# A PEER expert layer on one core: a second raw buffer for U blocks, and the low halves of V blocks moved from GpSimd to VectorE

## The chip, the cores and the metric

The kernel runs on 1 core of one Trainium2 chip. The metric is the device time of one execution in microseconds (us); less is better. Three runs of the kernel before took 3746.31, 3746.49 and 3755.15 us, a median of 3746.49 us.

The engines are called as the profile calls them: PE is TensorE (PEld its weight loads), DVE is VectorE, ACT is ScalarE, POOL is GpSimd, SP is SyncE, which here only issues DMAs.

## The reference

One layer of a hybrid backbone over 1024 tokens of 1024 channels: adaLN norm, one input projection, a Hyena long convolution beside grouped-query attention, an output projection, and then a PEER layer of single-neuron experts. The change concerns the PEER layer alone:

```python
def chunk(xc):                       # 128 tokens
    q = (xc @ wq).reshape(PEER_CHUNK, PEER_HEADS, 2, half)
    s1 = jnp.einsum('chd,hnd->chn', q[:, :, 0], keys1)
    s2 = jnp.einsum('chd,hnd->chn', q[:, :, 1], keys2)
    ...                              # top 16 of the 128x128 sums per head
    g = jax.nn.softmax(best, axis=-1)
    a = jnp.einsum('chkd,cd->chk', u_tab[eidx], xc)
    wgt = gelu(a) * g
    return jnp.einsum('chk,chkd->cd', wgt, v_tab[eidx])
```

There are 16384 experts, each a row of U and a row of V (1024 float32 numbers, 4 KB). Every token uses 128 of them (8 heads by 16).

## The kernel before

Up to about 1685 us the kernel does everything ahead of the experts. The rest of the program does the expert layer in two ways side by side.

**Dense experts, the main work** (`dense`). The first 640 tokens (`DT` = 5 tiles of 128) meet all 16384 experts. U and V are cut into 128 blocks of 128 experts, and four blocks (`CH`) make a chunk. For each block the kernel loads a transposed U block `ur` (512 KB, issued on SP), and splits it into a rounded high half `uh` on ACT (L90) and a low half `ul` = `ur` - `uh` on DVE (L91); both go to a function `split`. PE then forms the products with the tokens in three passes (high by high, high by low, low by high: L85 to L87), 48 matmuls of 320 columns a block. ACT puts a GELU on the result (`ga`), DVE multiplies it by the gate weights `gt` (L1000), and `wh` and `wl` are its halves. The function `values` loads the V block `vr` (512 KB) and splits it into `vh` (ACT) and `vl`. After four blocks, `products` forms the output of the chunk for each of the five tiles, 24 matmuls of 512 columns a tile, and DVE adds each half of it from PSUM to `acc` (L1022), ten additions a chunk.

The buffers matter here: one `ur` (`UR` = 1), one `vr`, two each of `uh` and `ul`, four each of `vh` and `vl` (`VH`). The constant `VG` = (0, 2) says on which engine `vl` is made: for blocks whose number is 0 or 2 modulo 4 on POOL, for the others on DVE.

**Gathered experts, the background.** For the other 384 tokens (tiles 5 to 7, list `E`) the rows of U and V are gathered by index. POOL issues 128 indirect DMAs a tile for U (`usweep`, L887; one row for each of 128 tokens, 512 KB) and 128 for V (`vrows`, L933). DVE takes the dot product of each U row with its token (L888) and adds each V row, weighted, to a sum in PSUM (L937). `topk` finds the indices. It also transposes them on PE into `eT`, for a function `vsweep`; the list `VD` = (5, 6, 7) sends all three tiles to `vrows`, so that `vsweep` is never run, and `eT` is not read.

`weave` writes background steps among the dense steps at a fixed ratio. The order that each engine then gets is made by the framework's scheduler, which plays the program through on estimated durations. Every engine works strictly in the order it got, and SP issues its DMAs in that order too: an instruction that waits holds up all that stand behind it.

Of the kernel before, what the change touches and what calls it, by code (L numbers as in the profile page):

```python
# [10 lines left out]
F32 = mybir.dt.float32  # L11
F32R = mybir.dt.float32r
I32 = mybir.dt.int32
# [4 lines left out]
PSUM = bass.MemoryType.PSUM  # L18
# [3 lines left out]
D = 1024  # L22
# [30 lines left out]
RUNS = _runs()  # L53
RW = 7
VB = 2
CH, WB, VH, GA, UR = 4, 4, 4, 1, 1
OB, GB = 4, 2
RB, RB0, RBR, MGB = 3, 2, 1.0, 4
O1DVE, OA = (0,), 1
BG0, BGR0 = 200, 2.4  # L60
VG = (0,2)
GB4, MGB4, OA4, OB4 = 2, 2, 1, 3
ND, DC = 2, 23
LR = 3
VD = (5, 6, 7)
BGR = 1.3
DT = 5

# [1 line left out]
def body(tc, d, out, dbg=None):  # L70
# [4 lines left out]
    def pool(name, bufs=1, space=None, stack=es, **kw):  # L75
        if space is not None:
            kw["space"] = space
        if space != DRAM:
            kw["reuse_waits"] = "tile"
        return stack.enter_context(tc.tile_pool(name=name, bufs=bufs, **kw))  # L80
# [12 lines left out]
    with es:  # L93
# [706 lines left out]
        def topk(i, v16, i16, p, res, ps, dense):  # L800
# [50 lines left out]
            efl = ef.rearrange("p h k -> p (h k)")  # L851
            if "eidx" in dbg:
                SY.dma_start(dbg["eidx"][i], efl)
            pt = ps.tile([128, 512], F32, name="ms")
            PE.transpose(pt[:, 0:128], efl, ident)
            if not dense:
                ei = res.tile([128, 128], I32, name=f"ei{i}", bufs=1)
                V.tensor_copy(ei, efl)
                eT = res.tile([128, 128], I32, name=f"eT{i}", bufs=1)
                V.tensor_copy(eT, pt[:, 0:128])  # L860
                tops[i] = gwl, ei, eT
                return
            PE.transpose(pt[:, 128:256], gwl, ident)
            nb = 1 if i == DT - 1 else 2
            gT = res.tile([128, 256], F32, name="gT", bufs=nb)
# [28 lines left out]
            V.tensor_tensor(gw, gw, a, OP.mult)  # L894
            ws[i] = gw

        def vsweep(i, tops, ws, p, gp, ms, ap, res, wdz):
            w, eT = ws[i], tops[i][2]
            pt = ms.tile([128, 512], F32, name="ms")
            PE.transpose(pt[:, :128], w, ident)  # L900
            acc = ap.tile([128, 2, 512], F32, name="acc")
            pv = pt[:, :128].rearrange("p (c t) -> p c t", c=4)
            wT = res.tile([128, 4, 32], F32, name="wT", bufs=1)
            V.tensor_copy(wT, pv)
            for th in range(8):
                V.memset(wdz, 0.0)
                V.tensor_copy(wdz[:, :, th * 4:128:33], wT[:, :, th * 4:th * 4 + 4])
                for tm in range(4):
                    tl = th * 4 + tm
                    vgs = [gp.tile([128, D], F32, name="row", bufs=RW) if c else p.tile([128, D], F32, name="vg", bufs=VB) for c in range(4)]  # L910
                    for c in range(4):
                        G.indirect_dma_start(out=vgs[c], out_offset=None, in_=d["v"], in_offset=bass.IndirectOffsetOnAxis(ap=eT[:, c * 32 + tl:c * 32 + tl + 1], axis=0))
                    lead = None
                    for h in range(2):
                        for c in (3, 0, 1, 2):
                            mm = PE.matmul(acc[c * 32:c * 32 + 32, h, :], wdz[:, c, tm * 32:tm * 32 + 32], vgs[c][:, h * 512:(h + 1) * 512],
                                           start=tl == 0, stop=tl == 31, tile_position=(0, c * 32))
                            if lead is None:
                                lead = mm
                            else:  # L920
                                tc.add_manual_dep(mm.ins, lead.ins.name, mybir.DependencyInfo(mybir.DependencyClass.NoSync, mybir.DependencyReason.DATA), reason="behind the last gather")
                    yield 1
            gt = [gp.tile([128, D], F32, name="row", bufs=RW) for _ in range(4)]
            gates(gt)
            final(i, acc.rearrange("p a b -> p (a b)"), gt[2], gt[3], gt, p)

        def vrows(i, tops, ws, p, gp, ap):

            w, ei = ws[i], tops[i][1]
            acc = ap.tile([128, 2, 512], F32, name="acc").rearrange("p a b -> p (a b)")  # L930
            for s_ in range(128):
                row = gp.tile([128, D], F32, name="h2" if i == 7 else "row", bufs=1 if i == 7 else RW) if s_ % 3 == 1 else p.tile([128, D], F32, name="vg", bufs=VB)
                G.indirect_dma_start(out=row, out_offset=None, in_=d["v"], in_offset=bass.IndirectOffsetOnAxis(ap=ei[:, s_:s_ + 1], axis=0))  # L933
                if s_ == 0:
                    V.tensor_scalar(acc, row, w[:, 0:1], None, OP.mult)
                else:
                    V.scalar_tensor_tensor(acc, row, w[:, s_:s_ + 1], acc, OP.mult, OP.add)  # L937
                if s_ % 4 == 3:
                    yield 1
            gt = [gp.tile([128, D], F32, name="row", bufs=RW) for _ in range(4)]  # L940
            gates(gt)
            final(i, acc, gt[2], gt[3], gt, p)
# [34 lines left out]
        def dense(hTh, hTl, gp):  # L977
# [4 lines left out]
            chunks = [list(range(b, min(b + CH, 128))) for b in range(0, 128, CH)]  # L982
            with ExitStack() as st:
                p = pool("de", 1, stack=st)
                ps = pool("deps", 5, PSUM, stack=st)
                acc = p.tile([128, DT, 2, 512], F32, name="acc")

                def weights(c):
# [79 lines left out]
        def gates(gt):  # L1068
            SY.dma_start(gt[0], modd[3:4, :].to_broadcast([128, D]))
            SY.dma_start(gt[1], d["fin_g"].to_broadcast([128, D]))  # L1070
# [43 lines left out]
        with ExitStack() as sg:  # L1114
# [19 lines left out]
            with ExitStack() as sk:  # L1134
# [6 lines left out]
                for _ in rest(0, 4, rps, rwp, tkv, ra, hq):  # L1141
                    pass
                v16, i16, hTh, hTl = ra
                ms = pool("ms", 1, PSUM, stack=sg, side="right")
                def weights_of(tiles, v16, i16, pools, on_act, gb):
                    bp, mg, tk, st_ = pools
                    for i in tiles:
# [22 lines left out]
                with ExitStack() as sb:  # L1170
                    for _ in weights_of(DD[4:], v16, i16, pools(sb, 4, MGB4), OA4, GB4):
                        pass
                gp = pool("gp", 1, stack=sg, side="right")
                sl = ExitStack()
                tk = pool("tk2", 1, stack=sl, side="right")
# [1 line left out]

                def background():
                    def tk_(i):
                        return topk(i, v16[:, i % 4], i16[:, i % 4], tk, res, ms, False)  # L1180

                    yield from tk_(E[0])
                    for i in E[1:]:
                        yield from alternate(tk_(i), first(us[0], 24))
                    sl.close()
                    vp = pool("vp", 1, stack=sg, side="right")
                    ap = pool("ap", 1, PSUM, stack=sg, side="right")
                    wdz = vp.tile([128, 4, 128], F32, name="wdz")
                    vs = [vsweep(i, tops, ws, vp, gp, ms, ap, res, wdz) for i in E if i not in VD]
                    vs += [vrows(i, tops, ws, vp, gp, ap) for i in VD]  # L1190
                    yield from us[0]
                    for j in range(len(E) - 1):
                        yield from alternate(us[j + 1], vs[j])
                    yield from vs[-1]
# [105 lines left out]
```

## Time and profile before

| what | value |
|---|---|
| median of three runs | 3746.49 us |
| the profiled execution: its own time | 3752.46 us |
| the profiled execution: span of the trace | 3750.7 us |
| mean granted TensorE clock | 0.949 |
| first `ur` issued, last `ur` issued | 1685.1 us, 3692.9 us |
| first, last U gather started | 1865.3 us, 3282.6 us |
| last V gather started | 3696.6 us |

The profile is of one execution. Busy time of an engine is the union of its instructions' spans; a group's row gives its count, its busy time, the mean time of one instruction, and then the idle time of the engine just before them with what ended it. In a list of waits, a row names the waiting engine and line, what it waited for, the total, how often, and the longest. Times within the span are counted from its start.

### The profile page before, as it was taken

What the parts mean: (1) busy time and instruction counts of PE and PEld (TensorE: products, weight loads), DVE (VectorE), ACT (ScalarE), POOL (GpSimd) and SP (SyncE); (2) the same over time, 40 slices, a digit from 0 to 9 for tenths busy, and PEclk for the clock granted to TensorE, in tenths of its full rate; (3) what the DMA queues carried; (4) which work ended last, traced back from release to release, by engine and by line L of the source; (5) the groups of instructions that cost most, each with busy time, mean ns of one, the idle gap of its engine ahead of it and who ended that gap; (6) DMA issues with size and microseconds to landing.
All of it is one profiled execution on the core that took longest, in us unless ns stands there. A gap on an engine that the chain in (4) does not pass through costs nothing.

```text
span 3750.7 us, 53277 instructions
## 1 busy us (share of the span) xinstructions
PE 3369.1 (90%) x19601; PEld 2948.2 (79%) x19601; DVE 2879.9 (77%) x5428; ACT 1445.1 (39%) x2966; POOL 1709.2 (46%) x1360
## 2 busy tenths in 40 slices
PE   5899999789999886998889998999999999799998
PEld 2787888567887676888778888988888888687887
DVE  4655554574446899999897989898898989787777
ACT  5543422446565268885511222222232222122222
POOL 0233133220421465104486767676576666544452
PEclk6999999899999998999989999999999999899999
DMA  4554355863322344434488999999999989888886
GB/s 164 176 165 153 129 202 167 294 226 117 110 85 65 104 141 163 167 141 142 165 305 307 322 327 329 337 344 324 335 342 331 325 317 326 286 286 285 264 281 210
DMA packets 334241, 868.31 MB, mean 232 GB/s; under 512 B 31777, under 2 KB 145377, under 8 KB 324764
## 3 DMA queue, kind: packets, MB, share of 16 engines
q0 software_dynamic: 123904, 453.04, 33.9%
q1 hardware_dynamic: 210076, 411.87, 32.4%
q8 instruction: 154, 2.52, 0.3%
q14 instruction: 107, 0.88, 0.1%
HBM read 777.63 MB, written 87.18 MB: 231 GB/s over the span
## 4 chain that ended last, share of the span: by engine, by line
DVE 23%; DMA 16%; PE 14%; issue 8%; POOL 3%; ACT 2%; SPq 0%; DVEq 0%; POOLq 0%; ACTq 0%
PE mm L85 5%; PE mm L86 4%; PE mm L87 4%; DMA vg<-in_v,ei 4%; DMA vr<-in_v 3%; DVE row L888 3%; DVE acc L937 3%; DMA row<-in_u,ei 3%; DMA ur<-in_uT 3%; DVE o L953 2%; DVE o L965 2%; DVE wl L91 1%; DMA h<-in_v,ei 1%; DVE o L963 1%; POOL row L887 1%
## 5 line engine op out<-in xcount | busy, mean ns | idle before, releaser
L85 PE MATMUL mm<-h2Th,uh 128*128 128x320 f32 x2048 | 644.7, 315 | 60.7 <-ACT uh L90 50.3
L87 PE MATMUL mm<-h2Th,ul 128*128 128x320 f32 x2048 | 638.5, 314 | 26.7 <-DVE ul L91 25.8
L86 PE MATMUL mm<-h2Tl,uh 128*128 128x320 f32 x2048 | 641.7, 314 | 0.0
L887 POOL DMA_INDIRECT row<-in_u,ei x384 | 500.4, 1303 | 192.9 <-issue 75.3
L85 PE MATMUL mm<-vh,wh 128*128 128x512 f32 x1280 | 500.6, 404 | 59.6 <-DVE acc L1022 35.9
L888 DVE SCALAR_TENSOR_TENSOR row<-row,h 128x1024 f32<-128x1024 f32 x384 | 508.1, 1341 | 25.1 <-DMA row<-in_u,ei 21.7
L86 PE MATMUL mm<-vl,wh 128*128 128x512 f32 x1280 | 504.3, 401 | 5.8 <-DVE vl L91 3.9
L87 PE MATMUL mm<-vh,wl 128*128 128x512 f32 x1280 | 497.4, 400 | 7.6 <-DVE wl L91 7.5
L85 PEld LDWEIGHTS mm<-h2Th,uh 128*128 128x128 f32 x2048 | 392.9, 192 | 68.6 <-ACT uh L90 56.0
L933 POOL DMA_INDIRECT vg<-in_v,ei x255 | 310.6, 1218 | 295.8 <-DVE acc L937 244.7
L87 PEld LDWEIGHTS mm<-h2Th,ul 128*128 128x128 f32 x2048 | 389.9, 191 | 34.1 <-DVE ul L91 32.1
L86 PEld LDWEIGHTS mm<-h2Tl,uh 128*128 128x128 f32 x2048 | 392.9, 192 | 1.6
L937 DVE SCALAR_TENSOR_TENSOR acc<-vg,gw,acc 128x1024 f32<-128x1024 f32 x252 | 323.3, 1283 | 60.8 <-DMA vg<-in_v,ei 55.7
L85 PEld LDWEIGHTS mm<-vh,wh 128*128 128x128 f32 x1280 | 247.7, 194 | 124.7 <-DVE acc L1022 46.3
L87 PEld LDWEIGHTS mm<-vh,wl 128*128 128x128 f32 x1280 | 248.3, 194 | 63.9 <-DVE wl L91 10.2
L86 PEld LDWEIGHTS mm<-vl,wh 128*128 128x128 f32 x1280 | 248.7, 194 | 57.2 <-DVE vl L91 5.6
L90 ACT CAST uh<-ur 128x1024 fp32r<-128x1024 f32 (+1 forms) x130 | 137.8, 1060 | 360.4 <-DMA ur<-in_uT 308.8
L90 ACT CAST vh<-vr 128x1024 fp32r<-128x1024 f32 x133 | 139.2, 1047 | 323.9 <-DMA vr<-in_v 207.6
L1040 ACT ACTIVATE ga<-mm 128x320 f32<-128x320 f32 x256 | 107.1, 436 | 395.8 <-PE mm L87 203.0
L91 DVE TENSOR_TENSOR ul<-ur,uh 128x1024 fp32r<-128x1024 f32 (+1 forms) x130 | 165.2, 1271 | 109.0 <-ACT uh L90 102.1
L1022 DVE TENSOR_TENSOR acc<-acc,mm 128x512 f32<-128x512 f32 x322 | 209.9, 680 | 42.3 <-PE mm L87 35.3
L90 ACT CAST wh<-ga 128x640 fp32r<-128x640 f32 (+2 forms) x136 | 94.7, 696 | 373.2 <-DVE ga L1000 232.2
(359 smaller groups left out, 7837.2 us busy)
## 6 DMA issues: line engine op xcount, KB each, us to landing
vr<-in_v SPq DMA_DIRECT2D x133, 512.0 KB
ur<-in_uT SPq DMA_DIRECT2D x128, 512.0 KB
gd<-gst SPq DMA_DIRECT2D x40, 1024.0 KB
gt<-gd SPq DMA_DIRECT2D x32, 1024.0 KB
wt<-in_ada_w SPq DMA_DIRECT2D x12, 2048.0 KB
cfr<-in_cf POOLq DMA_DIRECT2D x32, 512.0 KB
mt<-in_cf POOLq DMA_DIRECT2D x16, 1024.0 KB
mt<-in_ci POOLq DMA_DIRECT2D x16, 1024.0 KB
```

The costliest lines, as they stand in the source:

```text
L85: PE.matmul(ps, ah, bh, start=start, stop=False)
L86: PE.matmul(ps, ah, bl, start=False, stop=False)
L87: PE.matmul(ps, al, bh, start=False, stop=stop)
L90: S.copy(hi, src)
L91: (eng or V).tensor_tensor(lo, src, hi.bitcast(F32), OP.subtract)
L887: G.indirect_dma_start(out=ug, out_offset=None, in_=d["u"], in_offset=bass.IndirectOffsetOnAxis(ap=ei[:, s_:s_ + 1], axis=0))
L888: V.scalar_tensor_tensor(ug, ug, 1.0, h2, OP.mult, OP.mult, accum_out=a[:, s_:s_ + 1])
L933: G.indirect_dma_start(out=row, out_offset=None, in_=d["v"], in_offset=bass.IndirectOffsetOnAxis(ap=ei[:, s_:s_ + 1], axis=0))
L937: V.scalar_tensor_tensor(acc, row, w[:, s_:s_ + 1], acc, OP.mult, OP.add)
L953: V.tensor_tensor(o2, io128[:, None, :].to_broadcast([128, 4, 128]), i2T[:, ts_, None].to_broadcast([128, 4, 128]), OP.is_equal)
L1022: V.tensor_tensor(acc[:, i, h, :], acc[:, i, h, :], po, OP.add)
L1040: S.activation(ga[:, ts_], pa[:, :NS], AF.Gelu_apprx_tanh)
```

## The change

`UR` becomes 2: a second raw buffer for U blocks. `VG` becomes empty: all `vl` are made on DVE. For the tiles of `E`, `topk` no longer transposes the indices, and the unused `vsweep` goes, with its tile `wdz`; the PSUM pool `ms` is closed before the dense experts begin. The number of PSUM buffers of the dense experts gets a name, `PB`, and stays 5.

```diff
-CH, WB, VH, GA, UR = 4, 4, 4, 1, 1
+CH, WB, VH, GA, UR, PB = 4, 4, 4, 1, 2, 5
...
-VG = (0,2)
+VG = ()
...
-VD = (5, 6, 7)
...
-            pt = ps.tile([128, 512], F32, name="ms")
-            PE.transpose(pt[:, 0:128], efl, ident)
             if not dense:
                 ei = res.tile([128, 128], I32, name=f"ei{i}", bufs=1)
                 V.tensor_copy(ei, efl)
-                eT = res.tile([128, 128], I32, name=f"eT{i}", bufs=1)
-                V.tensor_copy(eT, pt[:, 0:128])
-                tops[i] = gwl, ei, eT
+                tops[i] = gwl, ei
                 return
+            pt = ps.tile([128, 512], F32, name="ms")
+            PE.transpose(pt[:, 0:128], efl, ident)
...
-        def vsweep(i, tops, ws, p, gp, ms, ap, res, wdz):
...
-                ms = pool("ms", 1, PSUM, stack=sg, side="right")
+                sm_ = ExitStack()
+                ms = pool("ms", 1, PSUM, stack=sm_, side="right")
...
+                sm_.close()
                 gp = pool("gp", 1, stack=sg, side="right")
...
-                    wdz = vp.tile([128, 4, 128], F32, name="wdz")
-                    vs = [vsweep(i, tops, ws, vp, gp, ms, ap, res, wdz) for i in E if i not in VD]
-                    vs += [vrows(i, tops, ws, vp, gp, ap) for i in VD]
+                    vs = [vrows(i, tops, ws, vp, gp, ap) for i in E]
```

What the two constants do is seen in the engines' order. Names carry a number for each buffer, which is 12 smaller in the changed kernel, and its lines have lower numbers: L1030 becomes L997 (`ur`), L1006 becomes L973 (`vr`), L994 becomes L961 (`gt`).

SP's queue around the start of a chunk in the middle of the dense experts, before; the chunk's four U blocks are `ur_25435`, `25505`, `25575` and `25645`, its gate weights `gt_25432`:

```order
L1030 DMA ur_25435<-in_uT 128x1024
L1006 DMA vr_25286<-in_v 128x1024
L994 DMA gt_25432<-gd16_84 128x16x128
L994 DMA gt_25432<-gd4_85 128x4x128
L1030 DMA ur_25505<-in_uT 128x1024
L1006 DMA vr_25499<-in_v 128x1024
L1030 DMA ur_25575<-in_uT 128x1024
L1006 DMA vr_25569<-in_v 128x1024
L1030 DMA ur_25645<-in_uT 128x1024
```

The same chunk in the changed kernel; its U blocks are `ur_25423`, `25493`, `25563` and `25633`, its gate weights `gt_25420`:

```order
L997 DMA ur_25423<-in_uT 128x1024
L973 DMA vr_25204<-in_v 128x1024
L997 DMA ur_25493<-in_uT 128x1024
L973 DMA vr_25274<-in_v 128x1024
L997 DMA ur_25563<-in_uT 128x1024
L997 DMA ur_25633<-in_uT 128x1024
L973 DMA vr_25487<-in_v 128x1024
L961 DMA gt_25420<-gd16_84 128x16x128
L961 DMA gt_25420<-gd4_85 128x4x128
L973 DMA vr_25557<-in_v 128x1024
```

All four U loads of a chunk now stand ahead of the load of its gate weights, where three of them stood behind it.

DVE's order at the end of the chunk before, where PE forms its products and DVE adds them up (L1022); `ul_25508` belongs to the second block of the next chunk:

```order
L1022 TENSOR_TENSOR acc_16779<-acc_16779,mm_25362 128x512
L888 SCALAR_TENSOR_TENSOR row_21417,a_19792<-row_21417,h2_19790 128x1024
L1022 TENSOR_TENSOR acc_16779<-acc_16779,mm_25376 128x512
L1022 TENSOR_TENSOR acc_16779<-acc_16779,mm_25390 128x512
L91 TENSOR_TENSOR ul_25508<-ur_25505,uh_25507 128x1024
L1022 TENSOR_TENSOR acc_16779<-acc_16779,mm_25404 128x512
L1022 TENSOR_TENSOR acc_16779<-acc_16779,mm_25418 128x512
```

The same place in the changed kernel, where that block is `ul_25496`, L885 and L904 are the dot products and the weighted additions of gathered rows, and `vl_25277` and `wl_25270` belong to the last block of the old chunk:

```order
L90 TENSOR_TENSOR ul_25496<-ur_25493,uh_25495 128x1024
L885 SCALAR_TENSOR_TENSOR row_21396,a_19780<-row_21396,h2_19778 128x1024
L904 SCALAR_TENSOR_TENSOR acc_19793<-vg_21171,gw5_17374,acc_19793 128x1024
L90 TENSOR_TENSOR wl_25200<-ga_25146,wh_25199 128x640
L90 TENSOR_TENSOR vl_25277<-vr_25274,vh_25276 128x1024
L904 SCALAR_TENSOR_TENSOR acc_19793<-vg_21174,gw5_17374,acc_19793 128x1024
L967 TENSOR_TENSOR ga_25216<-ga_25216,gt_24997 128x640
L885 SCALAR_TENSOR_TENSOR row_21399,a_19780<-row_21399,h2_19778 128x1024
L904 SCALAR_TENSOR_TENSOR acc_19793<-vg_21177,gw5_17374,acc_19793 128x1024
L885 SCALAR_TENSOR_TENSOR row_21402,a_19780<-row_21402,h2_19778 128x1024
L90 TENSOR_TENSOR wl_25270<-ga_25216,wh_25269 128x640
```

The low half of the next chunk's second U block has moved from among the ten additions to ahead of the last `wl` of the old chunk, and so ahead of all ten.

More of the change, by code (lines that the diff above doesn't have):

```diff
@@ L895, in usweep @@
             ws[i] = gw
-        def vsweep(i, tops, ws, p, gp, ms, ap, res, wdz):
[L898 to L925, printed above, removed]
         def vrows(i, tops, ws, p, gp, ap):
@@ L931, in vrows @@
             for s_ in range(128):
-                row = gp.tile([128, D], F32, name="h2" if i == 7 else "row", bufs=1 if i == 7 else RW) if s_ % 3 == 1 else p.tile([128, D], F32, name="vg", bufs=VB)
+                row = gp.tile([128, D], F32, name="h2" if i == E[-1] else "row", bufs=1 if i == E[-1] else RW) if s_ % 3 == 1 else p.tile([128, D], F32, name="vg", bufs=VB)
                 G.indirect_dma_start(out=row, out_offset=None, in_=d["v"], in_offset=bass.IndirectOffsetOnAxis(ap=ei[:, s_:s_ + 1], axis=0))
@@ L984, in dense @@
                 p = pool("de", 1, stack=st)
-                ps = pool("deps", 5, PSUM, stack=st)
+                ps = pool("deps", PB, PSUM, stack=st)
                 acc = p.tile([128, DT, 2, 512], F32, name="acc")
@@ L1179, in tk_ @@
                     def tk_(i):
-                        return topk(i, v16[:, i % 4], i16[:, i % 4], tk, res, ms, False)
+                        return topk(i, v16[:, i % 4], i16[:, i % 4], tk, res, None, False)
                     yield from tk_(E[0])
```

## The prediction

> **What bounds the kernel now.** I read the page first, for the engines over the whole span, then the busy time by stage, then PE's groups and the list of waits in the dense stage, then single lines with their shortest, middle and longest instruction.
>
> ```profile
> span 3750.7 us, 53277 instructions
> PE 3369.1 (90%) x19601; PEld 2948.2 (79%) x19601; DVE 2879.9 (77%) x5428; ACT 1445.1 (39%) x2966; POOL 1709.2 (46%) x1360
> ```
>
> Over the span PE is the busiest, but the change touches only the dense stage. By stage (columns: stretch, length, then busy time of PE, PEld, DVE, ACT, POOL, the granted clock, the share of the DMA engines, GB/s):
>
> ```profile
> 1685.00:1865.00 180.00, 158.82 (x991) 147.87 (x992) 163.77 (x528) 107.68 (x262) 77.54 (x121) 0.96 0.44 144
> 1865.00:3285.00 1420.00, 1311.43 (x7058) 1175.92 (x7057) 1247.49 (x1588) 323.86 (x464) 938.22 (x685) 0.96 0.91 324
> 3285.00:3690.00 405.00, 369.38 (x1978) 328.75 (x1977) 318.28 (x322) 98.82 (x142) 193.59 (x150) 0.97 0.83 277
> ...
> 2400.00:2600.00 200.00, 198.54 (x1097) 179.10 (x1096) 179.62 (x224) 46.32 (x66) 132.92 (x100) 1.00 0.96 344
> ```
>
> The long middle (1865 to 3285) has three engines near their limit at once: PE 92% busy (1311 of 1420), DVE 88% (1247), the DMA engines 91%. PE is idle for 108.6 us there and for 35.6 us in the late stage (405 less 369.4), together 144 us: no edit beside PE can give more than that here. The best 200 us show how it looks when nothing stalls: 1097 matmuls against 994 in the mean of the middle (7058 by 200 by 1/1420).
>
> What does PE wait for? Its groups, with the idle time before them and its cause:
>
> ```profile
> L85 PE MATMUL mm<-h2Th,uh 128*128 128x320 f32 x2048 | 644.7, 315 | 60.7 <-ACT uh L90 50.3
> L87 PE MATMUL mm<-h2Th,ul 128*128 128x320 f32 x2048 | 638.5, 314 | 26.7 <-DVE ul L91 25.8
> L85 PE MATMUL mm<-vh,wh 128*128 128x512 f32 x1280 | 500.6, 404 | 59.6 <-DVE acc L1022 35.9
> L87 PE MATMUL mm<-vh,wl 128*128 128x512 f32 x1280 | 497.4, 400 | 7.6 <-DVE wl L91 7.5
> ```
>
> The halves of U blocks cost PE 50.3 + 25.8 = 76.1 us, half of its idle time. DVE's late additions cost 35.9. And behind those halves, in the list of waits of the dense stage (who waited for whom: total, times, longest):
>
> ```profile
> ACT uh L90 <- DMA ur<-in_uT: 308.8, 50, 24.5
> POOL vl L91 <- ACT vh L90: 115.4, 28, 14.7
> DVE ul L91 <- ACT uh L90: 75.9, 23, 10.0
> DVE acc L937 <- DMA vg<-in_v,ei: 55.7, 41, 4.9
> DVE vl L91 <- ACT vh L90: 15.2, 13, 3.0
> DVE eT L860 <- PE ms L855: 7.3, 1, 7.3
> ...
> SPq L1030 <- DVE ul L91: 403.6, 87, 11.8
> ```
>
> The last row is from the waits of SP's queue in the middle and late stage. Read upwards it is one chain: SP can't issue the next `ur` until `ul` has released the only buffer; ACT then waits for the landing, 6.2 us in the mean of 50 waits; DVE stands at `ul` for 75.9 us, and PE behind both.
>
> **The second U buffer.** With it a load is issued one load earlier. From 1685.1 to 3692.9 us there are 128 loads:
>
> ```profile
> L1030 SPq DMA_DIRECT2D ur<-in_uT x128: 327/328/6318, 1685.1 to 3692.9; - x128
> ```
>
> that is one in 15.7 us. This lead is more than the mean wait of 6.2 us, though less than the longest, 24.5. Bounds of the gain: nothing, if what PE waits for is only exchanged for another late thing, and 76.1 us, if all of it goes. I take two thirds, 50 us, since the mean wait is covered two times over, and the rest stays for the longest waits and for `ul` behind other work of DVE. The same removal gives DVE back most of its 75.9 us at `ul`, and with that the extra work of the next part has room. In SP's queue all four loads of a chunk now stand ahead of `gt`, which itself waits for DVE's last multiplication; what is moved behind them are V loads, and they no longer stand behind an `ur` that waits for its buffer.
>
> **The low halves of V on DVE.** 67 subtractions move:
>
> ```profile
> L91 POOL TENSOR_TENSOR vl<-vr,vh x67: 2371/2422/3431, 1693.4 to 3688.2; 128x1024 fp32r<-128x1024 f32 x67
> L91 DVE TENSOR_TENSOR vl<-vr,vh x66: 1200/1219/1797, 1702.1 to 3678.4; 128x1024 fp32r<-128x1024 f32 x66
> L888 DVE SCALAR_TENSOR_TENSOR row<-row,h x384: 1202/1217/3826, 1876.8 to 3291.7; 128x1024 f32<-128x1024 f32 x192
> L1000 DVE TENSOR_TENSOR ga<-ga,gt x136: 279/817/3549, 1707.8 to 3717.1; 128x640 f32<-128x640 f32 x120, 128x512 f32<-128x512 f32 x8, 128x128 f32<-128x128 f32 x8
> ```
>
> DVE gets 67 by 1.219 = 82 us more. But look at the longest instructions: a dot product of 1.217 us sometimes takes 3.826, a gate multiplication of 0.817 takes 3.549. The excess is about one POOL subtraction (2.422). The groups' means, against these middles, say what it costs DVE in all:
>
> ```profile
> L888 DVE SCALAR_TENSOR_TENSOR row<-row,h 128x1024 f32<-128x1024 f32 x384 | 508.1, 1341 | 25.1 <-DMA row<-in_u,ei 21.7 <-issue 2.8
> L937 DVE SCALAR_TENSOR_TENSOR acc<-vg,gw,acc 128x1024 f32<-128x1024 f32 x252 | 323.3, 1283 | 60.8 <-DMA vg<-in_v,ei 55.7 <-issue 2.5 <-DVE wl L91 0.7
> L1000 DVE TENSOR_TENSOR ga<-ga,gt 128x640 f32<-128x640 f32 x120 | 110.9, 924 | 10.6 <-ACT ga L1040 10.4
> L91 DVE TENSOR_TENSOR wl<-ga,wh 128x640 fp32r<-128x640 f32 x120 | 107.8, 898 | 0.8 <-ACT wh L90 0.8
> ...
> L937 DVE SCALAR_TENSOR_TENSOR acc<-vg,gw,acc x26: 1277/1287/1290, 3599.9 to 3703.1; 128x1024 f32<-128x1024 f32 x26
> ```
>
> Dot products: 384 by (1341 - 1217) ns = 48 us; `ga`: 120 by (924 - 817) = 13; `wl`, of the same shape: 120 by (898 - 817) = 10. Together 71 us. The weighted additions (L937), whose sum lies in PSUM, show none of it (mean 1283, longest 1290 in the last row). If all of the 71 us belong to POOL's subtractions, DVE's net load rises by 82 - 71 = 11 us; if none does, by 82. I take 11, as the lengthening has the size of one POOL subtraction, and charge it at DVE's share of the middle, 0.88: 10 us.
>
> The Trainium skill, page "SBUF — State Buffer", section "Who interferes with whom", says that VectorE reading two inputs from SBUF and GpSimd reading SBUF exclude each other for a whole instruction. By it up to 67 by 2.422 = 162 us could have been taken from DVE, and the net would be a relief of 80 us instead of a load of 11; the trace's 71 us is less than half of that, since DVE is often at an instruction that does not compete, and I keep the trace's number.
>
> What waits for what is changed as well. POOL waited 115.4 us for `vh`, that is 1.72 us for each of its 67; DVE, which comes later to its own, waited 15.2 us for 66, or 0.23. The moved 67 wait on DVE between these: 15 us by the one, 115 us by the other. They will stand in DVE's order, so I take the 0.23, 15 us, at 0.88: 13 us. Behind such a wait stand `ul`, `wl` and the additions, and PE behind them.
>
> POOL loses 67 by 2.575 = 173 us of work and its waits at `vh`, and issues gathers earlier. DVE's idle time for gathered rows is 25.1 us for U and 55.7 for the largest V group, so the bound of the gain is about 80 us. Late V gathers cycle through three buffers, though, and wait for DVE to free them; I take 5 us.
>
> **The rest.** Without the transposes, DVE's 7.3 us wait for PE (`eT` row above) goes, in a stage where DVE is 91% busy (163.8 of 180): 7 us; the bounds are 0, if the wait was free time, and 7.3. The closed PSUM pool, `PB` and the removed function cost nothing: no instruction changes by them, and no wait for that bank stands in the list above.
>
> **The sum.** -50 + 10 + 13 - 5 - 7 = -39 us. The profiled execution took 3752.46 us, 6 us above the median; 3752.5 - 39 = 3713.5 by it, and by the median of the runs 3746.5 - 39 = 3707.5. I give 3707.
>
> DMA permits it: the middle moves 324 GB/s by 1420 us = 460 MB, and at the 344 GB/s of the best slice this takes 1337 us, 83 us less. The Trainium skill, page "DMA: Bandwidth & Descriptors", section "Where 436 GB/s comes from", has about 358 GB/s from HBM for one core when its neighbour streams too, an estimate of 1285 us for these bytes; no run here shows that rate.
>
> **The rivals.**
>
> *DVE becomes the bound, slower.* `vl` on DVE waits for late V loads as POOL's did. Place: DVE, at each `vl`, while one `vr` buffer still serves all. At 1.72 us each, 115 us, by 0.88 = 101 instead of 13: +88, so 3707 + 88 = 3795. It decides from (39 + 13) / (67 by 0.88) = 0.88 us a wait on. For it: all 133 now stand on an engine 88% busy. Against it: 0.23 us for the 66 that already do. Half way it is 3750.
>
> *The wait is only exchanged.* PE's U waits go, but the DMA engines at 0.91 deliver gathers later by as much, so DVE and PE stand elsewhere: the gain of 50 falls to about 10, 3747. For it: three engines within 4% of each other. Against it: 0.96 and 344 GB/s over 200 us, with PE 99% busy.
>
> *More comes free.* All 76.1 us of U waits go, and half of the 80 us of gather waits: -76 + 10 + 13 - 40 - 7 = -100, so 3647. For it: POOL's 173 us of work and 102 us of waiting vanish:
>
> ```profile
> L91 POOL TENSOR_TENSOR vl<-vr,vh 128x1024 fp32r<-128x1024 f32 x67 | 172.6, 2575 | 101.9 <-ACT vh L90 100.8 <-issue 0.4
> ```
>
> Against it: DVE, not POOL, is what the gathers' buffers wait for.
>
> **How the numbers follow.** My forecast (3670 to 3732 by itself) has 0.58, the exchanged wait 0.17, the slower rival 0.15, the larger gain 0.10. The least difference that a measurement of this kernel tells from none is about 0.3%, 11 us: under 3735 is faster, over 3758 slower. Faster: 0.58 + 0.10 + a few hundredths of the exchanged wait = 0.71; same: 0.13, the rest of it and the rival's half way; slower: 0.16. For the range I leave out the slower rival above 3768 and the larger gain below 3650: 3650 to 3768.
>
> **What would show it.** Right: ACT's wait for `ur` falls from 308.8 us to under 100, PE's idle before L85 and L87 of U from 76 to under 30; the dot products' mean falls from 1341 to about 1225 ns and their longest under 2 us; DVE's share of the middle rises to 0.90 or more. Wrong: DVE's wait at `vl` for `vh` above 60 us, or PE's wait for `acc` (35.9 us) above 80, which would mean that DVE is late with everything; or ACT's wait for `ur` stays, which would mean that the loads are late by bandwidth and not by the buffer.

## The result and the profile after

The changed kernel takes 3665.22 us in the median of 4 runs (3659.73 to 3668.98), beside 3746.40 us for the kernel before, measured with it: a ratio of 0.978 (95% interval 0.976 to 0.980), 81 us less. The forecast was 39 us less; the time lies inside the range and outside the forecast's own 3670 to 3732 us.

The first two lines of the page, and the busy time by stage (columns as in the prediction; the middle is cut at 3200 us, since everything now stands earlier):

```profile
span 3661.7 us, 53279 instructions
PE 3337.6 (91%) x19598; PEld 2927.3 (80%) x19598; DVE 2865.3 (78%) x5493; ACT 1440.6 (39%) x2966; POOL 1566.7 (43%) x1292
...
1685.00:1865.00 180.00, 159.14 (x1002) 148.42 (x1002) 172.09 (x562) 107.25 (x262) 67.98 (x124) 0.95 0.50 164
1865.00:3200.00 1335.00, 1272.10 (x6978) 1145.08 (x6979) 1224.06 (x1617) 321.13 (x462) 847.37 (x637) 0.98 0.95 346
3200.00:3600.00 400.00, 368.69 (x1989) 328.95 (x1988) 320.89 (x334) 96.52 (x141) 158.51 (x133) 0.98 0.84 275
```

In the middle DVE's share rose from 0.88 to 0.92 (1224 of 1335), the DMA engines' from 0.91 to 0.95, and the granted clock from 0.96 to 0.98. The 346 GB/s of this whole stretch are what the best 200 us of before had (344).

PE's groups, each with the idle time before it and its main cause:

```profile
L84 PE MATMUL mm<-h2Th,uh 128*128 128x320 f32 x2048 | 636.2, 311 | 22.3 <-ACT ga L1007 11.2
L86 PE MATMUL mm<-h2Th,ul 128*128 128x320 f32 x2048 | 634.3, 311 | 11.4 <-DVE ul L90 11.3
...
L84 PE MATMUL mm<-vh,wh 128*128 128x512 f32 x1280 | 494.0, 400 | 49.1 <-DVE acc L989 19.9
L85 PE MATMUL mm<-vl,wh 128*128 128x512 f32 x1280 | 499.9, 397 | 13.8 <-DVE vl L90 13.8
L86 PE MATMUL mm<-vh,wl 128*128 128x512 f32 x1280 | 488.9, 398 | 16.6 <-DVE wl L90 16.6
```

Of the 76.1 us before the U products 11.3 us at `ul` and at most 11.1 us at `uh` are left (half of the first row's idle time is for `ga`). Before the V products PE waits no less than it did, 80 us by the three rows against 73 (59.6, 7.6 and 5.8, the last for `vl`), and for more kinds of things. The waits of the others, and the dot products (shortest, middle, longest in ns):

```profile
ACT uh L89 <- DMA ur<-in_uT: 9.0, 2, 8.6
ACT vh L89 <- DMA vr<-in_v: 425.3, 59, 23.1
DVE vl L90 <- ACT vh L89: 52.9, 25, 9.9
...
L885 DVE SCALAR_TENSOR_TENSOR row<-row,h x384: 1208/1219/1490, 1867.9 to 3195.5; 128x1024 f32<-128x1024 f32 x192
L885 DVE SCALAR_TENSOR_TENSOR row<-row,h 128x1024 f32<-128x1024 f32 x384 | 462.5, 1221 | 13.6 <-DMA row<-in_u,ei 12.3
```

ACT's wait for `ur` fell from 308.8 to 9.0 us and now stands at `vr` (207.6 us before); PE's own wait for `vh` is 18.8 us in both kernels. The dot products lost their long ones.

**A ledger for PE.** Ends of matmuls are modelled in the trace, so idle rows can hide lost time. Starts are recorded. Where nothing stalls, the U matmuls (320 columns) of the dense stage start 147 ns apart and the V matmuls (512 columns) 227 ns; what single gaps exceed this by (10 ns or more), summed, is PE's lost time. The wait of 11 us ahead of the very first U product, which all of them have, is left out. For the kernels that differ in the two constants:

| kernel (`UR`; low halves on POOL, block number modulo 4) | lost at U, us | lost at V, us | span less both, us | median, us | ratio to before |
|---|---|---|---|---|---|
| before (1; 0, 2) | 109 | 119 | 3522 | 3746 | 1 |
| after (2; none) | 34 | 116 | 3512 | 3665 | 0.978 (0.976 to 0.980) |
| e1 (1; 0, 2) | 109 | 116 | 3525 | 3748 | 1.000 (0.998 to 1.003) |
| e2 (2; 0, 2) | 31 | 156 | 3522 | 3707 | 0.989 (0.983 to 0.994) |
| e3 (1; none) | 86 | 103 | 3522 | 3711 | 0.991 (0.987 to 0.994) |
| e4 (2; all) | 40 | 227 | 3530 | 3800 | 1.015 (1.010 to 1.021) |
| e5 (2; 1, 3) | 30 | 183 | 3518 | 3735 | 0.997 (0.995 to 0.999) |
| e6 (2; 3) | 26 | 154 | 3510 | 3687 | 0.984 (0.980 to 0.988) |
| e9 (2; 0) | 28 | 127 | 3512 | 3673 | 0.980 (0.976 to 0.984) |
| e10 (2; 2) | 31 | 184 | 3514 | 3715 | 0.990 (0.986 to 0.994) |
| e13 (1; 0) | 67 | 113 | 3522 | 3706 | 0.988 (0.983 to 0.993) |
| e14 (1; 2) | 75 | 145 | 3519 | 3740 | 0.997 (0.995 to 1.000) |

The column "span less both" stays within 20 us while the span moves by 135: what PE loses at these two places is most of what the changes move. From before to after it is 75 us at U and 3 at V, 78 of the 89 us by which the span is shorter. (The kernel before was measured anew beside each group of experiments, with medians of 3740 to 3753 us, so kernels of different groups are compared by ratio; 1% is 37.5 us.)

### The profile page after: what moved, and what is told of

Same layout as the page of the kernel before. It is cut to its first block, busy times and chain, and to the rows that moved or that the text cites. A ratio compares the mean times of both kernels' runs of the same rounds, so it can differ in the third digit from the quotient of the medians.

```text
span 3661.7 us, 53279 instructions
## 1 busy us (share of the span) xinstructions
PE 3337.6 (91%) x19598; PEld 2927.3 (80%) x19598; DVE 2865.3 (78%) x5493; ACT 1440.6 (39%) x2966; POOL 1566.7 (43%) x1292
## 4 chain that ended last, share of the span: by engine, by line
PE 24%; DVE 22%; DMA 11%; issue 6%; POOL 1%; ACT 1%; SPq 0%; DVEq 0%; POOLq 0%; ACTq 0%
PE mm L84 8%; PE mm L85 8%; PE mm L86 8%; DMA vr<-in_v 3%; DMA vg<-in_v,ei 3%; DVE acc L904 3%; DVE row L885 3%; DMA h<-in_v,ei 2%; DVE o L920 2%; DVE o L932 2%; DVE wl L90 1%; DVE vl L90 1%; DMA row<-in_u,ei 1%; DVE o L930 1%; DVE ul L90 1%
## 5 line engine op out<-in xcount | busy, mean ns | idle before, releaser
L84 PE MATMUL mm<-h2Th,uh 128*128 128x320 f32 x2048 | 636.2, 311 | 22.3 <-ACT ga L1007 11.2
L86 PE MATMUL mm<-h2Th,ul 128*128 128x320 f32 x2048 | 634.3, 311 | 11.4 <-DVE ul L90 11.3
L884 POOL DMA_INDIRECT row<-in_u,ei x384 | 522.8, 1361 | 209.0 <-DVE row L885 87.4
L85 PE MATMUL mm<-vl,wh 128*128 128x512 f32 x1280 | 499.9, 397 | 13.8 <-DVE vl L90 13.8
L86 PE MATMUL mm<-vh,wl 128*128 128x512 f32 x1280 | 488.9, 398 | 16.6 <-DVE wl L90 16.6
L900 POOL DMA_INDIRECT vg<-in_v,ei x255 | 320.9, 1259 | 375.7 <-DVE acc L904 293.8
L885 DVE SCALAR_TENSOR_TENSOR row<-row,h 128x1024 f32<-128x1024 f32 x384 | 462.5, 1221 | 13.6 <-DMA row<-in_u,ei 12.3
L86 PEld LDWEIGHTS mm<-h2Th,ul 128*128 128x128 f32 x2048 | 385.9, 189 | 15.3 <-DVE ul L90 14.6
L904 DVE SCALAR_TENSOR_TENSOR acc<-vg,gw,acc 128x1024 f32<-128x1024 f32 x252 | 323.5, 1284 | 44.8 <-DMA vg<-in_v,ei 43.7
L937 PE MATMUL ms<-o,o 128*128 128x128 f32 x1280 | 181.1, 290 | 29.5 <-ACT o L925 12.4
L90 DVE TENSOR_TENSOR vl<-vr,vh 128x1024 fp32r<-128x1024 f32 x133 | 163.2, 1227 | 53.0 <-ACT vh L89 52.9
```

The lines of the kernel that those rows point to most:

```text
L84: PE.matmul(ps, ah, bh, start=start, stop=False)
L85: PE.matmul(ps, ah, bl, start=False, stop=False)
L86: PE.matmul(ps, al, bh, start=False, stop=stop)
L90: (eng or V).tensor_tensor(lo, src, hi.bitcast(F32), OP.subtract)
L884: G.indirect_dma_start(out=ug, out_offset=None, in_=d["u"], in_offset=bass.IndirectOffsetOnAxis(ap=ei[:, s_:s_ + 1], axis=0))
L885: V.scalar_tensor_tensor(ug, ug, 1.0, h2, OP.mult, OP.mult, accum_out=a[:, s_:s_ + 1])
```

## The experiments

**One part at a time, e1 to e4.** Two theories: A, the second buffer carries the gain that was not forecast; B, it comes from what POOL's subtractions held up.

```diff
 e1:  UR = 1, VG = (0, 2)      only the rest of the change
 e2:  UR = 2, VG = (0, 2)      the second buffer
 e3:  UR = 1, VG = ()          the low halves
 e4:  UR = 2, VG = (0, 1, 2, 3)
```

> The changed kernel with both constants set back (UR = 1, VG = (0, 2)): only the unused function, the transposes of the gathered tiles and the early closing of the PSUM pool remain. Theory A (the second U buffer carries the gain; a stall of PE costs its idle time and then a stretch at a lower granted clock): 3740 us, within 0.3% of before, PE's waits for U halves near 76 us and the granted clock of the long middle 0.96 as before. Theory B (taking POOL's subtractions out of DVE's and the gathers' way carries the gain): the same 3740. Theory C (the gain comes from the transposes and the memory layout that the removed function changes): under 3700.

> The changed kernel with VG = (0, 2): two U buffers, POOL still makes the low halves of half of the V blocks. Theory A: 3675 us or less, at least 65 of the 81 us; PE's waits for U halves under 30 us, the granted clock of the long middle up from 0.96 to 0.97 or 0.98, dot products still at a mean of 1.34 us. Theory B: 3715 or more, since DVE still loses its 70 us to POOL's subtractions.

> The changed kernel with UR = 1: one U buffer, all low halves of V on DVE. Theory A: 3735 to 3755 us, no gain that can be told, PE's waits for U halves still 70 us or more, the granted clock of the long middle 0.96; dot products at a mean of 1.22 us. Theory B: 3695 or less.

> Two U buffers, and all low halves of V on POOL (VG = (0, 1, 2, 3)), the opposite move. DVE issues 66 subtractions of 1.22 us fewer than before and is lengthened by 133 of POOL's. Theory A: DVE's load is about the same either way (82 us of instructions against 71 us of lengthening for each 67), so 3665 to 3690 us. Theory B: each subtraction on POOL costs, so 3710 or more, and dot products at a mean of 1.45 us.

Measured: e1 3748.37 us, the rest of the change is worth nothing. e2 3706.81 us: the buffer alone is worth 1.2%, 43 us. e3 3711.39 us: the low halves alone are worth 1.0%, 36 us, where the prediction had charged 18. e4 3800.46 us. So neither theory has it alone; the buffer's part was near its forecast and that of the low halves had the wrong sign.

In e2 the U stalls are gone (31 us lost at U), but 40 us more are lost at V than in e1. Two of PE's waits and a stretch of the stages show where:

```profile
PE mm L85 <- DVE vl L90: 47.5, 11, 35.7
PE mm L84 <- ACT vh L89: 25.8, 6, 14.9
...
3620.00:3640.00 20.00, 2.50 (x5) 1.50 (x5) 10.27 (x9) 1.22 (x2) 7.14 (x8) 0.50 0.89 309
3640.00:3660.00 20.00, 0.00 (x0) 0.00 (x0) 10.82 (x9) 0.00 (x0) 7.51 (x8) 0.50 0.74 235
```

One wait of 35.7 us and one of 14.9 stand near the end: PE does nothing for 20 us while DVE adds gathered rows. The chain of waits of e2 says why (start, length, what):

```profile
3660.44 4.94 DMA h<-in_v,ei
3665.48 1.30 DVE acc L904
3666.80 1.23 DVE row L1043
3669.20 1.23 DVE vl L90
```

The last low half of V stands behind the last gathered row in DVE's order, which the scheduler fixed before the run. In e2, 25 weighted additions stand behind the last `ul`, in the changed kernel none; the last V gather starts at 3660.4 us against 3597.0. At chunk 30 of 32, e2 was 14 us ahead of the changed kernel, and at the end 47 us behind it: with two buffers all that the low halves of blocks 0 and 2 cost on POOL was lost in this tail. With one buffer there is no such tail: 2 weighted additions stand behind the last `ul` in the kernel before, none in e1 and 2 in e3. There e1 falls behind e3 bit by bit, by 2 us at chunk 4, 18 at chunk 16 and 35 at chunk 30.

**Does a subtraction on POOL cost only by that tail? e5, e6, e9, e10.**

```diff
-VG = ()
+VG = (1, 3)     # e5;  e6: (3,);  e9: (0,);  e10: (2,)
```

> The changed kernel, but POOL again subtracts the low halves of two dense V blocks in four: those with b%4 of 1 and 3, where the kernel before and the run with the second U buffer alone had 0 and 2. POOL's work is the same 64 subtractions as in that run, whose median was 3706.81 us; in the order of instructions 4 gathered V rows are left behind the last dense U block, against 25 there and 0 in the changed kernel. Theory T1 (what a POOL subtraction costs is that it holds back the gathers, and with the second U buffer the bill is a tail of gathered rows after the dense blocks, 36 + 15 us of PE's waits in that run): no tail here, 3660 to 3682 us, and PE waits less than 15 us for rows after 3600 us. Theory T2 (each subtraction on POOL costs where it stands, by lengthened DVE instructions, late V low halves and late gathers): 3697 to 3712 us, as with blocks 0 and 2, the loss being spread over the dense stage.

> The changed kernel with one low half in four (b%4 of 3) on POOL, 32 subtractions. No gathered row is left behind the last dense block in the order. T1 (only the tail costs): the changed kernel's time, 3660 to 3672 us, or a few us less, as DVE is relieved of 32 x 1.2 us. T2 (each subtraction costs where it stands): half of the 37 to 42 us that two in four cost, 3680 to 3690 us.

Measured: e5 3734.65 us (10 runs), e6 3687.22 us. Both have hardly a tail and both take longer than the changed kernel, so the tail is not all. PE's waits of e5, then of e6:

```profile
PE mm L85 <- POOL vl L90: 59.2, 15, 7.3
PE mm L85 <- POOL vl L90: 40.6, 12, 6.6
```

In a chunk PE takes about 7 us for the U products of each block and some 31 for its V products (27 where nothing stalls), which need all four V blocks. The last block's low half, made on POOL in 2.4 us and not in 1.2, comes too late.

> The changed kernel with one low half in four on POOL, that of the blocks with b%4 of 0: 32 subtractions, as in the run with b%4 of 3 (3687.22 us, where PE waited 40.6 us for POOL's low halves, since that block is the last that V's products need). In the order of instructions 7 gathered V rows are left behind the last dense U block. T1 (a subtraction on POOL costs only by the gathered rows it leaves for the end, or where PE waits for that low half itself): PE's wait for POOL's low halves under 10 us and 7 rows x 2.1 us left over: 3665 to 3682 us. T2 (each costs 0.65 us where it stands): 32 x 0.65 = 21 us, 3682 to 3692 us.

> The same with b%4 of 2: again 32 subtractions, but 24 gathered rows are left behind the last dense U block. T1: as with b%4 of 0, and (24 - 7) x 2.1 = 36 us more, 3697 to 3715 us, all of the loss after 3520 us. T2: the same time as with b%4 of 0, within 8 us.

Measured: e9 3673.13 us, not to be told from the changed kernel; e10 3715.31 us, 42 us above e9, near T1's 36 and not as T2 said. But in the traces 43 of the 61 us between e9 and e10 arise after chunk 30 and 19 before it, so "all after 3520 us" failed. The other 19 stand beside this, DVE's groups of e9 and then of e10:

```profile
L885 DVE SCALAR_TENSOR_TENSOR row<-row,h 128x1024 f32<-128x1024 f32 x384 | 486.3, 1283 | 17.1 <-DMA row<-in_u,ei 16.6
L90 DVE TENSOR_TENSOR ul<-ur,uh 128x1024 fp32r<-128x1024 f32 x115 | 144.2, 1254 | 18.1 <-ACT uh L89 18.1
L90 DVE TENSOR_TENSOR wl<-ga,wh 128x640 fp32r<-128x640 f32 (+1 forms) x128 | 102.3, 799 | 1.4 <-ACT wh L89 1.4
...
L885 DVE SCALAR_TENSOR_TENSOR row<-row,h 128x1024 f32<-128x1024 f32 x384 | 473.4, 1249 | 21.0 <-DMA row<-in_u,ei 20.9
L90 DVE TENSOR_TENSOR ul<-ur,uh 128x1024 fp32r<-128x1024 f32 x115 | 156.1, 1357 | 12.9 <-ACT uh L89 12.5
L90 DVE TENSOR_TENSOR wl<-ga,wh 128x640 fp32r<-128x640 f32 (+1 forms) x128 | 111.6, 872 | 1.4 <-ACT wh L89 1.4
```

Block 0's subtractions lengthen mostly dot products (mean 1283 ns against 1221 in the changed kernel), block 2's also `ul` and `wl`, which PE waits for. By the starts in the traces, of e9's 29 subtractions in chunks 4 to 30 18 fall into the first two blocks of a chunk and 11 into the late V products ahead of them; of e10's 29, 25 fall into the first 12 us of the fourth block, where PE is about to need the last `wl`, `vh` and `vl`.

**With one buffer, e13 and e14.**

```diff
-VG = ()
+VG = (0,)       # e13, with UR = 1;  e14: (2,), with UR = 1
```

> One U buffer, and POOL subtracts one low half in four, of the blocks with b%4 of 0; in the order no gathered row is left behind the last dense U block. With one buffer the time was 3748.37 us with two in four on POOL and 3711.39 us with none. T3 (each POOL subtraction delays gathers that DVE waits for, in proportion): 3725 to 3735 us. T4 (with one buffer too, only a place where POOL's work is late for somebody costs, and block 0 is early): 3708 to 3718 us. The difference to the same with two U buffers (3673.13 us) is then what the second buffer is worth where no tail takes part of it back: 52 to 62 us by T3, 35 to 45 us by T4; the prediction said 50.

> The same with b%4 of 2; 3 gathered rows are left behind the last dense U block, against 24 with two U buffers (3715.31 us). T1 (with two buffers the 42 us between b%4 of 2 and of 0 are the tail of gathered rows alone): here the two stand within 10 us of each other. Rival (block 2 itself is the dearer place for POOL, tail or not): 30 us or more above the run with b%4 of 0.

Measured: e13 3706.32 us, e14 3740.01 us (10 runs). T3 is wrong and T4 nearer: block 0 on POOL costs nothing against e3, though e13 lies 2 us under T4's range, and the second buffer is worth 31 us there and not 35 to 45. T1 as the only price of block 2 is wrong: with no tail to speak of block 2 still costs 34 us more than block 0. The mean distance from the start of the fourth U block of a chunk to the next chunk, which holds the V products, is 38.64 us in e13 and 39.71 in e14 (chunks 4 to 30); 32 times the difference are 34 us. DVE's idle time for gathered rows does not tell the two apart (99 and 97 us).

**POOL's work without its result, e11 and e16 to e18.** POOL makes subtractions into a scratch tile that nobody reads, four of 256 elements in each chosen block below 92; DVE keeps all low halves. In e11 they wait for nothing, in the others for a high half. The scratch tile takes the space of two late tiles, `ga4` and `gt4`.

```diff
+  if b % 4 == 0 and b < 92:              # e16;  e17: b % 4 == 2;  e18: from uh, after split(uh, ul, ur)
+      for q in range(4):
+          dum = p.tile([128, 256], F32, name="g4", bufs=1)
+          s_ = vh.bitcast(F32)[:, 256 * q:256 * q + 256]
+          G.tensor_tensor(dum, s_, s_, OP.subtract)
```

> The changed kernel, and beside it POOL makes subtractions that nobody reads: for the 46 dense blocks with b%4 of 0 or 2 below 92, four of 256 elements each from a constant tile into a scratch tile, without a wait for a high half. DVE keeps all low halves, and no gathered row is left behind the last dense U block. If POOL's mere occupancy and the lengthening of DVE's dot products beside it cost (T2): 46 x 0.65 us or more, 3690 to 3705 us. If not (T1): 3662 to 3675 us, though the mean of the dot products rises above 1260 ns.

> The changed kernel; in the 23 blocks with b%4 of 0 below 92 POOL also makes four subtractions of 256 elements from the block's high half of V into a scratch tile that nobody reads. One gathered row is left for the end in the order. They wait for the same high half as block 0's low half did. T5 (a POOL subtraction costs what it lengthens of wl, ga and ul on DVE, and nothing where it lengthens dot products of gathered rows): these three lengthened by less than 6 us, 3660 to 3675 us. Rival T6 (POOL's occupancy costs by delaying gathers, wherever it stands): 23 x 0.65 to 1.1 us or more, 3680 to 3692 us.

> The same with the 23 blocks with b%4 of 2, no row left for the end. T5: wl, ga and ul lengthened by 20 to 32 us, and the time higher by about as much, 3685 to 3700 us. T6: the same time as beside block 0. Rival T7 (what block 2 cost was its low half coming late for PE or its place in DVE's order): no loss, 3660 to 3672 us, since nobody waits for this work.

> The same in the 23 blocks with b%4 of 0, but POOL subtracts from the block's high half of U, for which DVE's ul waits too, so that the two stand beside each other. T5: ul lengthened by 15 to 30 us and the time higher by about as much, 3680 to 3695 us, though the work on POOL is the same as in the run beside block 0's V. T6: the same time as there. T7: 3660 to 3672 us.

Measured: e11 3719.25 us (0.992), but it doesn't answer: as its work waits for nothing, the scheduler put 131 of its 200 pieces before 1865 us, and all that it lost against the changed kernel (60 us) was lost before chunk 4. e16 3684.97 us (0.985), e17 3718.84 us (0.994), e18 3690.13 us (0.985): 28, 61 and 27 us above the changed kernel by the ratios. Lost at V were 137, 172 and 139 us. So T7 is wrong: beside block 2 it costs 33 us more than beside block 0, though nobody waits for the result. T6 is wrong that the place is indifferent, and right that this work costs something in each of the three places, 27 us at least. (In e9 nothing of it was seen, perhaps because DVE was relieved at the same time of 32 by 1.22 = 39 us; no run separates the two.) T5's price is wrong as well: against the changed kernel `ul`, `ga`, `wl` and `vl` were lengthened together by about 2, 16 and 16 us, yet e18 costs as much as e16 and not as e17. What stands between e16 and e17 in the traces is POOL's place in time:

```profile
L981 POOL TENSOR_TENSOR g<-vh 128x256 f32<-128x256 f32 x88 | 88.1, 1002 | 43.4 <-ACT vh L89 39.5
L981 POOL TENSOR_TENSOR g<-vh 128x256 f32<-128x256 f32 x88 | 79.4, 902 | 4.3 <-ACT vh L89 0.3
```

In e16 POOL is there early and waits for the high half, at the head of a chunk; in e17 it comes with the fourth block. The stretch from the start of the fourth U block to the next chunk takes 38.99 us in e16, 40.05 in e17 and 38.82 in e18 in the mean; 32 times the difference of the first two are 34 us, so the loss lies there, as in e14. Why that place costs 33 us more than e18's, which in the middle is 2.6 us earlier in the same block (5.7 and 8.3 us behind its start), stays open.

**A sixth bank, e7 and e12, and a part of the low halves on POOL, e15.** After the change PE waits for sums (`acc`), for `wl` and `vl`. Theory C: such a wait costs more than its length, by the clock behind it.

```diff
-CH, WB, VH, GA, UR, PB = 4, 4, 4, 1, 2, 5
+CH, WB, VH, GA, UR, PB = 4, 4, 4, 1, 2, 6      # e7
...
+  if c == 20: banks[5] = pool("deps2", 1, PSUM, stack=st)    # e12: every sixth sum goes there
...
-  split(vh, vl, vr, G if b % 4 in VG else V)
+  split(vh, vl, vr, G if b % 4 == 0 and b < 64 else V)       # e15
```

> The changed kernel with six instead of five banks of PSUM for the sums of the dense V blocks. PE's wait for DVE's accumulation (the acc row beside V's matmuls, 19.9 us in the changed kernel) falls below 10 us. If an idle us of PE is worth more than itself, because the granted clock drops after it (theory C): 3640 to 3655 us. If it is worth itself: 3652 to 3660 us. If DVE, 0.92 busy in the dense stage, sets the pace and PE would only wait elsewhere: 3662 to 3668 us, with the wait moved to the rows of vl, wl and ul.

> The changed kernel with a sixth bank for the sums of the dense blocks only from chunk 20 on, in a pool of its own, so that the start of the dense blocks waits for nothing (with six banks from the beginning that start came 123 us later, and the blocks from chunk 4 to the end then took 48 us less). From chunk 24 on the changed kernel takes 520 us for eight chunks, with six banks 492 us. Theory C (PE's waits for sums are worth more than their length, by the granted clock behind them): 3630 to 3650 us. Rival (DVE, 0.92 busy, only gives its wait to another place): 3655 to 3668 us.

> The changed kernel with POOL taking the low halves of the blocks with b%4 of 0 below 64: 16 subtractions in the first half, where in the run with all 32 the chunks stood 12 to 19 us ahead of the changed kernel. In the order 6 gathered rows are left for the end. T1 by its own price (6 rows x 2.1 us against 16 x 1.2 us less on DVE): 3650 to 3665 us; if DVE's idle time takes it all up, 3665 to 3680 us, as with 32.

Measured: e7 3693.02 us (0.986). The same stretch in the changed kernel and in e7:

```profile
1685.00:1815.00 130.00, 118.93 (x722) 109.77 (x723) 122.70 (x428) 75.67 (x181) 44.22 (x86) 0.95 0.49 159
1685.00:1815.00 130.00, 51.97 (x254) 47.20 (x255) 119.51 (x493) 69.34 (x209) 53.93 (x110) 0.65 0.30 110
```

PE has 52 us of work in 130, and its first U product starts at 1815.9 us, right behind the last of the small products of the stage before (`ms`): the sixth bank is presumably one that this stage still holds. The dense blocks begin 123 us later. From chunk 4 on e7 is 48 us faster. e12 has the bank only from chunk 20: 3666.38 us (0.976, 0.971 to 0.981), no difference to the changed kernel, with 524 us for its last eight chunks against 520. So the bank is not what made e7's blocks fast; PE's wait for `acc` went from 20.0 to 15.3 us, and that for `vl` from 13.8 to 18.4, as the rival said. In e7's order 56 gathered rows more stand ahead of chunk 5 than in the changed kernel, and 36 more ahead of chunk 21. Its dot products began 38 us earlier (1830 us) and its chunk 5 came 80 us later, so these rows were done in time that the dense blocks lost, and part of that time probably came back later. e15: 3664.72 us (0.976, 0.971 to 0.981), the same, where its two theories meet. No version beat the changed kernel by more than the noise.

**The clock behind a wait, e8.**

> No part of the computation: bursts of 96 matmuls of 128x128 by 128x320 as the dense stage has them, with PE held between bursts by one subtraction behind 0, 1, 3, 7 or 15 additions of 1024 elements on DVE (12 waits of each length, 8 of the longest, some 1.6 to 20 us), and 480 or more matmuls without a wait before each group. Theory C (a wait lowers the granted clock of the matmuls behind it): 1.00 in the stretches without waits, below 1.00 in those with them; the lost time per wait, mean spacing of matmuls in a burst above that of the stretches without waits times 96, is over 1 us after waits of 3 us and more. Rival (the clock follows something else, such as load or heat): the spacing of the matmuls in a burst is the same whatever the wait before it, or lower after long waits.

```profile
PE   7999989889988889977777897556657964543489
...
PEclk9999999999988889998888998777778986766689
...
L98 PE MATMUL mm<-hTh,uf 128*128 128x320 f32 x1792 | 605.8, 338 | 378.6 <-DVE uf L112 378.6
L98 PE MATMUL mm<-hTh,uh 128*128 128x320 f32 x1280 | 397.5, 311 | 20.3 <-ACT uh L105 13.2
```

The granted clock (second row) falls where PE (first row) has waits. From the starts of the matmuls, 96 to a burst:

| from the last start before the wait to the first after it, us | bursts | lost in the burst behind it, mean us |
|---|---|---|
| 2.15 | 11 | 1.0 (1.6 behind seven, 0.1 behind four) |
| 3.41 | 11 | 2.0 |
| 5.93 | 11 | 2.2 |
| 10.97 | 11 | 2.4 |
| 21.05 | 7 | 2.6 |

Theory C is right as to the clock: around a wait the clock records show a stretch at 0.50 of 3.4, 6.8, 10.2, 13.7 or 23.9 us, the longer ones in part within the wait itself, and in its rest behind the wait matmuls start up to 267 or 430 ns apart and not 147. A wait of 2 to 3.3 us costs PE half as much again. It did not make e12 faster, as nothing was saved there.

## Why the prediction was right or wrong, by its own steps

- **The second U buffer, -50.** Right within 7 us where POOL works as before or not at all: 1.2% or 43 us (e1 to e2) and 1.3% or 47 us (e3 to after). In the two other pairs it is 0.8% or 28 to 31 us (e13 to e9, e14 to e10). Mechanism and marks held: ACT's wait for `ur` 9.0 us, PE's at U about 22. PE lost 39 to 78 us less at U when POOL's part is held; in all four pairs V's products took 13 to 40 us of it back.
- **The low halves of V on DVE, +10 and +13, and POOL freed, -5: this is the step that failed.** Put at +18 together, it measured -36 us with one buffer and -40 with two (1.0% and 1.1%). Of its terms, DVE's net load was sound: from e2 to after dot products, `ga`, `wl` and `ul` give back 39 + 22 + 9 + 9 = 79 us of busy time, and `vl` takes 74. The waits at `vl` for `vh` were undersized: they grew from 6.8 to 52.5 us, by 46 and not by 15, yet they stayed under the mark of 60, and PE waits only 13.8 us for DVE's `vl`. The term that broke is "POOL freed, I take 5". These are DVE's groups of gathered rows with the idle time before them, in e2 and then in the changed kernel (its dot products are shown above):

```profile
L885 DVE SCALAR_TENSOR_TENSOR row<-row,h 128x1024 f32<-128x1024 f32 x384 | 501.0, 1321 | 27.6 <-DMA row<-in_u,ei 27.0
L904 DVE SCALAR_TENSOR_TENSOR acc<-vg,gw,acc 128x1024 f32<-128x1024 f32 x252 | 323.5, 1284 | 73.1 <-DMA vg<-in_v,ei 70.8
L904 DVE SCALAR_TENSOR_TENSOR acc<-h,gw,acc 128x1024 f32<-128x1024 f32 x43 | 55.4, 1288 | 27.4 <-DMA h<-in_v,ei 26.9
...
L904 DVE SCALAR_TENSOR_TENSOR acc<-vg,gw,acc 128x1024 f32<-128x1024 f32 x252 | 323.5, 1284 | 44.8 <-DMA vg<-in_v,ei 43.7
L904 DVE SCALAR_TENSOR_TENSOR acc<-h,gw,acc 128x1024 f32<-128x1024 f32 x43 | 55.3, 1286 | 24.6 <-DMA h<-in_v,ei 24.4
```

DVE's idle time for gathered rows fell by 48 us with two buffers (128 to 80, e2 to after) and by 47 with one (119 to 72, e1 to e3), where the term had 5. Its bound of about 80 us was short too: with the two smaller V groups the kernel before has 104 us of it. The 5 leaned on the three buffers of late V gathers and did not ask when the last row is done, against the last dense block. How the idle time became time of the kernel is shown with two buffers alone: in e2 the rows ended last. The -36 us with one buffer came without a tail; there the place of POOL's work decides (next point), and why it does so stays open.
- **What the step did not have at all:** a POOL subtraction's price goes by where it stands. Block 0 on POOL costs nothing net (e9, e13), block 2 costs 25 us with one buffer and 45 with two (e3 to e14, after to e10; most of the 45 is tail), block 3 makes PE wait 40.6 us for it (e6). The kernel before had 0 and 2, so most of its 36 us is block 2's. The Trainium skill (page "SBUF — State Buffer", section "Who interferes with whom") says that a VectorE instruction with two inputs in SBUF and a GpSimd instruction that reads SBUF contend for a shared pair of ports, which is an exclusive lock. The traces agree, as an instruction is held by up to a whole subtraction; the sum over 68 in the kernel before is 82 us, near the 71 that the prediction kept. But this sum does not give the time: in e17 and e18 `ul`, `ga`, `wl` and `vl`, which PE waits for, were held by 16 us together in each, and the kernels lost 61 and 27 us.
- **The rest, -7.** Nothing: e1 stands at 1.000 (0.998 to 1.003). The term's lower bound, 0, was the right value.
- **"No edit beside PE can give more than that here" (144 us).** The gain of 81 us did not pass it, but the bound was no bound: by starts PE lost 215 us in the same stretch (1865 to 3690 us). A part of the rest is the clock behind waits, which is not idle time: 1 less the granted clock, summed over the time from 1865 us on, is 75 us before and 40 after, some of it within the waits themselves.
- **The rivals.** *DVE becomes the bound* and *the wait is only exchanged* did not come, the first because the waits were 0.4 us for each `vl` (52.9 by 133), under its point of 0.88. *More comes free* (3647) was nearest in kind: it had half of the gather waits go, 40 of 80 us, and from e2 to after 48 of 128 went.

Each mark of "what would show it" came out right, and the size was still half: the marks tested the buffer and the lengthening, none tested when the gathered rows end.

## What to carry to other kernels

When two streams share an engine, work out for each which of them ends last, and price an edit by what it does to that one: 25 gathered rows left behind the last dense block made PE wait 51 us, which no mean wait showed. A subtraction moved from a helper engine is not priced by its length: the same 32 cost nothing beside one block and 25 to 45 us beside another, and the lengthening of the instructions beside it did not predict which; so try more than one place. And measure PE's losses by the starts of matmuls, not by its idle rows.

## What the runs showed of the hardware that was not expected

In e8, waits of PE of only 2.0 us brought the granted clock to 0.50 in 7 of 11 cases, longer ones always, and 96 matmuls behind them took 1.0 to 2.6 us longer in the mean. The Trainium skill (page "TensorE: Matmul & The Clock Gate", Part 1) tells of a window of about 3.4 us by which the clock is set, and of half rate after an idle one; the stretches at 0.50 are multiples of 3.4 us, as by that window, but a wait well below one window was enough here. POOL's 256-element subtractions took 0.9 to 1.0 us in the mean, four of them 3.6 to 4 us where one of 1024 took 2.4 to 2.6, so the pieces are dearer than the whole. A weighted addition with its sum in PSUM was not lengthened by any of them (mean 1281 to 1284 ns for the largest group in all of these kernels). And a gather's issue on POOL takes longer beside some work of DVE: in the changed kernel, from 1865 us on, the 24 issues of a gather with no DVE instruction beside them took 0.94 us in the mean, 102 beside weighted additions with the sum in PSUM 0.94 as well, and 323 beside DVE instructions with two inputs in SBUF 1.54 us (beside them for over 80% of their time).
